# A decoder trunk whose first matmul group opens by channel tiles, with all tokens in one step

## The chip, the cores and the metric

The kernel runs on one core of a Trainium2 chip. A core has a matrix engine (TensorE, PE in the profile), a vector engine (DVE), a scalar engine (ACT), a general engine (POOL), and a queue engine (SP) that issues most transfers. Each engine works through its own instructions in the order in which they were written, and waits on semaphores for the others. The metric is the time of the program on the device in microseconds (us), lower is better.

## The reference

Two decoder layers with macaron feed-forward blocks on 512 tokens of 1024 channels, all in float32:

```
def swiglu(x, w_in, w_out):
    g, u = jnp.split(x @ w_in, 2, axis=-1)
    return (jax.nn.silu(g) * u) @ w_out

for i in range(2):
    h = h + 0.5 * swiglu(rms_norm(h, ffn1_norm[i]), ffn1_w_in[i], ffn1_w_out[i])
    hn = rms_norm(h, mix_norm[i])
    h = h + (recurrent_mixer(hn, ...) if i == 0 else spatial_gating_mixer(hn, ...))
    h = h + 0.5 * swiglu(rms_norm(h, ffn2_norm[i]), ffn2_w_in[i], ffn2_w_out[i])
return rms_norm(h, final_norm)
```

The hidden width is 2816 = 22 tiles of 128. The change concerns the first swiglu of layer 0 alone, up to the point where its hidden blocks are handed on.

## The kernel before

**Numbers in two parts.** Every float32 matmul operand is split into a rounded high part and the rest: ACT copies the high part (`hi` for activations, `whi` for weights), DVE subtracts it and keeps the rest (`lo`, `wlo`). A product is three matmuls: whi with hi, whi with lo, wlo with hi. A weight block, loaded into one of eight `raw` buffers of 128x1024, is split once by `Sub.split`; there are four buffers each for `whi` and `wlo`.

**Seven products.** Most matrix products are done on 2x2 blocks in a seven-product scheme (`seven`, lines 336 to 418): the left side has quarters A11, A12, A22, A21 (two token halves, two channel halves) and the sums S1 = A21 - A22, S2, S4, S3 formed from them on DVE. Products come in the order P1 (A11), P2 (A12), P5 (S1), P6 (S2), P3 (S4), P7 (S3), Q4 (A22), each in two steps of twelve matmuls.

**Steps.** All products of the whole kernel stand in one list, `subs`. The loop at the end (lines 1444 to 1460) goes through it; for step i it runs the work hooked to its phase "pre", splits weights some steps ahead (`ahead`, otherwise three), runs "mid" and "rest", issues loads for buffers that have come free (`load_more`), emits the step's matmuls, and then "end", the step's own follow-up and "late". This fixes the order on every engine.

**The opening.** The hidden width is dealt out as a plain pair of two tiles ("p", `pair_plain`) and chunks of four tiles (`chunk`). The pair is computed without the seven products: for each token half, A12 and A11 (or A22 and A21) times the weights. Its steps 0 to 7 are the first of the kernel: (A12, first 256 channels), (A12, second), (A11, ...), (A11, ...), then the same four weight blocks again for A22 and A21. In this opening the operands are made on the way: x is transposed on PE (`turn`, through L265), its high and low part are taken from PSUM with the gain of the norm (`parts`), and the plain value is kept for the sums (`value`). The hooks at lines 1420 to 1436 place this work, the squares for the norm (`squares`, ACT) and its reciprocal root (`rstd`: mean on DVE, root on ACT, Newton step on DVE). `first.rest(1, None)` hooks the forming and splitting of S1, S2, S4 and S3, counted from step 1. The row scale 1/rms is applied only after the matmuls, in the pair's `silu` and `post` and in the chunk's follow-ups.

Step 8 begins the chunk: P1 in steps 8 and 9, P2 in 10 and 11, P5 in 12 and 13, P6 in 14 and 15, P3 in 16 and 17, P7 in 18 and 19. When P3's second step is done, DVE makes the chunk's hidden block (two instructions `c<-C,c` and two `c<-c,rt,c`), and PE transposes it after the following step (`left_blocks`); in the profile these transposes are `e<-ident,c` of L265. Those of the pair's hidden block are `e<-ident,h`.

**Loads.** x comes by five transfers, the pair's weights by ten (the first block in halves), all from SP in the order written at lines 1355 to 1362. At most eight loads are under way, by the eight semaphores that they use in turn. P5's weights are the sum of two blocks: SP loads one, POOL adds the other by an accumulating transfer (L137).

**Before the first matmul** PE runs dummy matmuls (`warm_up`): five, and two behind each of the first two transposes.

Of the kernel before, what the change touches and what calls it, by code (L numbers as in the profile page):

```python
# [52 lines left out]
def trunk(ctx: ExitStack, tc: tile.TileContext, a: dict, out: bass.AP):  # L53
# [29 lines left out]
    def f32(t):  # L83
        return t.bitcast(F32)
# [26 lines left out]
    class Raw:  # L111


        halves = False
# [35 lines left out]
    class Sub:  # L150
# [16 lines left out]
            self.tile.used()  # L167
            self.tile = None

        def split(self, vector=False):  # L170
# [11 lines left out]
            for q in ((slice(0, 1), slice(1, 2)) if self.raw.halves else (slice(0, k),)):  # L182
                if vector:
                    nc.vector.tensor_copy(self.hi[:, q, :], src[:, q, :])
                else:
                    act(self.hi[:, q, :], src[:, q, :], AF.Copy)
                tt(self.lo[:, q, :], src[:, q, :], f32(self.hi[:, q, :]), ALU.subtract)
            if self.then is not None:
                self.raw.add(self.then)
            self.raw.used()  # L190
# [533 lines left out]
        seven(in_block(w_in, lambda n: n * DFF + f0 * P, w), [[0, 1], [2, 3]], x_left(), w,  # L724
              dict(P1=p1, P2=p2, P5=p5, P6=p6, P3=p3, P7=p7, Q4=q4), own=first, spare=aux if first else bank)

    def pair_plain(w_in, f0, group, first=False):


        w, st, ht = 2 * P, {}, {}  # L730
        raw = {}
        for k in (1, 0):
            for h in range(2):
                raw[k, h] = PairRaw(w_in, k * 512 + h * 256, f0)
                raws.append(raw[k, h])

        def bank_of(half, s):
            if (half, s) not in st:
                st[half, s] = bank("p")
            return st[half, s]  # L740

        def product(sub, half, left, h, between=None):

            sq = [(s, q) for q in range(2) for s in range(2)]
            for i, (s, q, m) in enumerate([(s, q, m) for m in range(3) for s, q in sq] if first and h else
                                          [(s, q, m) for q in range(2) for m in range(3) for s in range(2)] if first else
                                          [(s, q, m) for s, q in sorted(sq) for m in range(3)]):
                if i == 8 and between is not None:
                    between()
                z = S.z[h].hl[left][m == 1][:, q * H + s * P : q * H + (s + 1) * P]  # L750
                nc.tensor.matmul(bank_of(half, s), z, (sub.lo if m == 2 else sub.hi)[:, q, :],  # L751
                                 start=left[2] == "2" and (h, q, m) == (0, 0, 0),
                                 stop=left[2] == "1" and (h, q, m) == (1, 1, 2))

        def silu(half, s):
            t = 2 * half + s
            ht[t] = slot(name="s1")[:, :w]
            act(ht[t], st[half, s][:, :w], AF.Silu, scale=S.rt[:, t : t + 1])

        def post(half):  # L760
            for s in range(2):
                ps, t = st[half, s], 2 * half + s
                if t not in ht:
                    silu(half, s)
                o = slot(name="h")[:, :w]
                stt(o, ps[:, w:], S.rt[:, t : t + 1], ht[t], ALU.mult, ALU.mult)
                ht[t] = o
            left_blocks(group, ht, half, 7 if first else 2)

        at0 = len(subs)  # L770
        for i, (half, left) in enumerate(((0, "A12"), (0, "A11"), (1, "A22"), (1, "A21"))):
            for h in range(2):
                def mm(sub, half=half, left=left, h=h):
                    product(sub, half, left, h, opening["A11"] if first and (left, h) == ("A12", 1) else None)

                end = None
                if (left, h) == ("A11", 1):
                    end = (lambda: (hook(at0 + 7, "rest", lambda: (silu(0, 0), silu(0, 1))),
                                    hook(at0 + 8, "mid", lambda: post(0)))) if first else lambda: post(0)
                elif (left, h) == ("A21", 1):  # L780
                    end = (lambda: hook(at0 + 9, "rest", lambda: post(1))) if first else lambda: post(1)
                subs.append(Sub(raw[1 - i, h], mm, end) if i < 2 else Again(subs[at0 + 2 * (i - 2) + h], mm, end))

    class PairRaw(Raw):


        def __init__(self, w_in, r0, f0):
            super().__init__(None, [P, 2, 512])
            self.w_in, self.r0, self.f0 = w_in, r0, f0

        def fetch(self):
            for q in ((slice(0, 1), slice(1, 2)) if self.halves else (slice(0, 2),)):
                for b, base in enumerate((0, DFF)):
                    c0 = base + self.f0 * P
                    ws = self.w_in[self.r0 + q.start * P : self.r0 + q.stop * P, c0 : c0 + 256]
                    nc.sync.dma_start(out=self.v[:, q, b * 256 : (b + 1) * 256],
                                      in_=ws.rearrange("(k p) c -> p k c", p=P))

    def ffn(w_in, w_out, norm):
        f0 = 0  # L800
        for i, sizes in enumerate(FF_PARTS):
            groups, p0 = [], f0
            for n in sizes:
                if n == "p":
                    groups.append(Group(1))
                    pair_plain(w_in, f0, groups[-1], not subs)
# [556 lines left out]

    warm = cp.tile([P, T], mybir.dt.bfloat16, tag="warm", name="warm")
# [23 lines left out]
    first = BlockNorm(V_F1)  # L1388
    S.z = first.g

    def turn(i, name, where=None):
        src, _ = first.src(i, name)
        opening[i, name] = first.g[i].turn(src, where)

    def parts(i, name):
        first.g[i].direct(name, opening[i, name], first.src(i, name)[1])

    def value(i, name, vector=False):

        g, ps, gains = first.g[i], opening.pop((i, name)), first.src(i, name)[1]  # L1400
        if name == "A21" or not vector:
# [7 lines left out]
    turn(0, "A12")  # L1409
    warm_up(2, 512)  # L1410
    turn(1, "A12")
    warm_up(2, 512)
    parts(0, "A12")
    subs[0].split()
    parts(1, "A12")
    subs[1].split()
    value(0, "A12")
    value(1, "A12")
    opening["A11"] = lambda: (turn(0, "A11"), turn(1, "A11"))
    for n, phase, fn in ((0, "late", vec_rest),  # L1420
                         (2, "pre", lambda: (subs[2].split(True), parts(0, "A11"), parts(1, "A11"))),
                         (2, "pre", lambda: (subs[3].split(), value(0, "A11", True), value(1, "A11", True))),
                         (2, "end", lambda: (turn(0, "A22", bank), turn(1, "A22", bank))),
                         (3, "pre", lambda: (parts(0, "A22"), parts(1, "A22"))),
                         (3, "mid", lambda: (value(0, "A22"), value(1, "A22", True))),
                         (3, "end", lambda: (turn(0, "A21"), turn(1, "A21"))),
                         (4, "mid", lambda: (parts(0, "A21"), parts(1, "A21"))),
                         (4, "rest", lambda: (value(0, "A21"), value(1, "A21")))):
        hook(n, phase, fn)
    squares(4, "rest", "A11")  # L1430
    squares(5, "rest", "A12")
    squares(6, "rest", "A22")
    squares(6, "rest", "A21")
    rstd(6, (0, "rest"), (0, "rest"), (1, "pre"))
    first.rest(1, None)
# [51 lines left out]
```

## Time and profile before

| | us |
|---|---|
| median of 3 runs (1622.64 to 1623.0) | 1622.69 |
| the profiled execution, its time | 1622.86 |
| its span, first to last instruction | 1621.2 |
| PE busy in the span | 1608.2 |
| DVE busy | 1373.8 |
| ACT busy | 1036.8 |
| granted TensorE clock, mean | 0.999 |

How to read the rows below. The timeline gives start, length, engine, line, operation, output <- inputs and count; what stands in brackets is the engine's idle time ahead of the row and what ended it. PEld is the loading of a matmul's stationary operand. Matmuls overlap each other, so a group's length is more than its pitch times the count. The chain of waits gives start, length and what the end of the program waited for at that time; for back-to-back matmuls its pieces are the pitch. The view of stretches gives the busy time of each engine in a stretch and the number of its instructions.

### The profile page before, as it was taken

What the parts mean: (1) busy time and instruction counts of PE and PEld (TensorE: products, weight loads), DVE (VectorE), ACT (ScalarE), POOL (GpSimd) and SP (SyncE); (2) the same over time, 40 slices, a digit from 0 to 9 for tenths busy, and PEclk for the clock granted to TensorE, in tenths of its full rate; (3) what the DMA queues carried; (4) which work ended last, traced back from release to release, by engine and by line L of the source; (5) the groups of instructions that cost most, each with busy time, mean ns of one, the idle gap of its engine ahead of it and who ended that gap; (6) DMA issues with size and microseconds to landing.
All of it is one profiled execution on the core that took longest, in us unless ns stands there. A gap on an engine that the chain in (4) does not pass through costs nothing.

```text
span 1621.2 us, 20840 instructions
## 1 busy us (share of the span) xinstructions
PE 1608.2 (99%) x7451; PEld 1327.0 (82%) x7451; DVE 1373.8 (85%) x1839; ACT 1036.8 (64%) x1504; POOL 221.8 (14%) x201
## 2 busy tenths in 40 slices
PE   9999999999999999999999999999999999999998
PEld 7888888888888888888888888888888788888886
DVE  6898888888998787877887978878978988879778
ACT  7656556658776556556775565566886766565665
POOL 2111111100010111111101111111211011111110
PEclk9999999999999999999999999999999999999999
DMA  9776876943383786876838768768877557686693
GB/s 275 183 168 166 210 179 158 214 126 105 92 208 86 176 217 156 209 168 158 206 86 192 168 162 212 181 154 208 217 192 191 155 120 192 167 208 159 161 206 100
DMA packets 164695, 279.29 MB, mean 172 GB/s; under 512 B 11520, under 2 KB 38000, under 8 KB 164592
## 3 DMA queue, kind: packets, MB, share of 16 engines
q1 hardware_dynamic: 115088, 184.84, 36.2%
q0 software_dynamic: 47712, 91.30, 33.8%
q10 hardware_dynamic: 1792, 1.84, 0.4%
q8 instruction: 58, 0.95, 0.2%
q14 instruction: 45, 0.37, 0.1%
HBM read 275.84 MB, written 2.10 MB: 171 GB/s over the span
## 4 chain that ended last, share of the span: by engine, by line
PE 94%; DVE 2%; ACT 2%; issue 1%; DMA 0%; SPq 0%; DVEq 0%; ACTq 0%
PE A L365 14%; PE A L366 14%; PE A L367 14%; PE C L366 7%; PE C L367 7%; PE C L365 7%; PE p L751 5%; PE B L365 4%; PE B L367 4%; PE B L366 4%; PE e L265 3%; PE r L225 2%; PE r L223 2%; PE r L224 2%; PE Q L367 1%; PE Q L365 1%
## 5 line engine op out<-in xcount | busy, mean ns | idle before, releaser
L96 ACT ACTIVATE whi<-raw 128x1024 fp32r<-128x1024 f32 (+1 forms) x536 | 553.2, 1033 | 388.0 <-PE A L366 103.9
L87 DVE TENSOR_TENSOR wlo<-raw,whi 128x1024 fp32r<-128x1024 f32 (+1 forms) x537 | 639.7, 1194 | 181.6 <-ACT whi L96 180.3
L365 PE MATMUL A<-whi,hi 128*128 128x512 f32 x1016 | 404.1, 398 | 0.0
L367 PE MATMUL A<-wlo,hi 128*128 128x512 f32 x1016 | 396.9, 391 | 0.0
L366 PE MATMUL A<-whi,lo 128*128 128x512 f32 x1016 | 396.5, 390 | 0.0
L367 PEld LDWEIGHTS A<-wlo,hi 128*128 128x128 f32 x1016 | 190.8, 188 | 41.6 <-DVE wlo L87 0.3
L366 PEld LDWEIGHTS A<-whi,lo 128*128 128x128 f32 x1016 | 191.1, 188 | 38.6 <-DVE lo L87 0.8
L365 PEld LDWEIGHTS A<-whi,hi 128*128 128x128 f32 x1016 | 190.9, 188 | 37.5
L366 PE MATMUL C<-whi,lo 128*128 128x512 f32 x560 | 218.7, 391 | 0.9 <-DVE lo L87 0.8
L365 PE MATMUL C<-whi,hi 128*128 128x512 f32 x560 | 218.5, 390 | 0.0
L367 PE MATMUL C<-wlo,hi 128*128 128x512 f32 x560 | 218.1, 389 | 0.0
L137 POOL DMA_DIRECT2D raw<-in_ffn_w_in_dram x82 | 98.8, 1205 | 741.1 <-DVE raw L87 524.5
L137 POOL DMA_DIRECT2D raw<-in_ffn_w_out_dram x72 | 83.0, 1160 | 378.7 <-DVE wlo L87 148.7
L87 DVE TENSOR_TENSOR raw<-raw,raw 128x1024 f32<-128x1024 f32 (+1 forms) x108 | 129.7, 1201 | 1.1 <-DMA raw<-in_ffn_w_out_dram 0.6
L87 DVE TENSOR_TENSOR lo<-a,hi 128x512 fp32r<-128x512 f32 (+1 forms) x188 | 123.1, 663 | 3.7 <-ACT hi L96 3.3
L366 PEld LDWEIGHTS C<-whi,lo 128*128 128x128 f32 x560 | 105.1, 188 | 24.7 <-DVE lo L87 3.2
L96 ACT ACTIVATE hi<-a 128x512 fp32r<-128x512 f32 (+1 forms) x188 | 112.4, 601 | 17.5 <-DVE a L87 14.3
L365 PEld LDWEIGHTS C<-whi,hi 128*128 128x128 f32 x560 | 105.2, 188 | 21.8
L367 PEld LDWEIGHTS C<-wlo,hi 128*128 128x128 f32 x560 | 105.2, 188 | 21.7
L96 ACT ACTIVATE c<-A 128x512 f32<-128x512 f32 x132 | 77.4, 594 | 56.3 <-PE A L367 55.9
L365 PE MATMUL B<-whi,hi 128*128 128x512 f32 x280 | 112.1, 400 | 0.0
L367 PE MATMUL B<-wlo,hi 128*128 128x512 f32 x280 | 109.4, 391 | 0.0
(161 smaller groups left out, 2106.3 us busy)
## 6 DMA issues: line engine op xcount, KB each, us to landing
raw<-in_ffn_w_in_dram SPq DMA_DIRECT2D x162, 512.0 KB, 4.4
raw<-in_ffn_w_out_dram SPq DMA_DIRECT2D x100, 512.0 KB, 5.3
raw<-in_ffn_w_in_dram POOLq DMA_DIRECT2D x82, 512.0 KB, 7.5
raw<-in_ffn_w_out_dram POOLq DMA_DIRECT2D x60, 512.0 KB, 8.1
raw<-in_sg_w_in_dram SPq DMA_DIRECT2D x20, 512.0 KB, 6.4
raw<-in_rec_w_in_dram SPq DMA_DIRECT2D x16, 512.0 KB, 3.8
raw<-in_ffn_w_in_dram SPq DMA_DIRECT2D x30, 256.0 KB, 5.0
raw<-in_sg_w_in_dram POOLq DMA_DIRECT2D x12, 512.0 KB, 7.8
```

The costliest lines, as they stand in the source:

```text
L87: nc.vector.tensor_tensor(out=o, in0=x, in1=y, op=op)
L96: nc.scalar.activation(out=o, in_=x, func=f, **k)
L137: nc.gpsimd.dma_start(out=self.v, in_=src, accum_op=ALU.add)
L223: nc.tensor.matmul(ps, wh, xh, start=start, stop=False)
L224: nc.tensor.matmul(ps, wh, xl, start=False, stop=False)
L225: nc.tensor.matmul(ps, wl, xh, start=False, stop=stop)
L265: nc.tensor.transpose(ps[:, o : o + P], src(q, s), ident)
L365: nc.tensor.matmul(ps, zh, wh, start=fresh and i == 0, stop=False, **k)
L366: nc.tensor.matmul(ps, zl, wh, start=False, stop=False, **k)
L367: nc.tensor.matmul(ps, zh, wl, start=False, stop=end, **k)
L751: nc.tensor.matmul(bank_of(half, s), z, (sub.lo if m == 2 else sub.hi)[:, q, :], start=left[2] == "2" and (h, q, m) == (0, 0, 0), stop=lef ...
```

## The change

The opening is dealt out anew. Instead of one token half and 256 channels, a step takes one channel tile of 128 and all 512 tokens: eight steps, each with one weight block of 128x512 (gate and up half), for both token halves. The four accumulators of the pair (two per half) live through all eight steps. The channel tiles come in the order 4, 5, 6, 7, 0, 1, 2, 3, so that the two tiles of a pair of steps use the same two transposed blocks.

- Loads: x in eight transfers of 256 KB, each followed by the two transfers of 128 KB of one weight block; 24 instead of 15.
- Warm-up: five, then three and a half dummy matmuls behind the first transpose.
- `between(n)`, behind the first two matmuls of step n, makes the operands of later matmuls: the transpose of unit n+1, its parts, the split of the next weights, the value of unit n-1, and in steps 1 to 6 the squares.
- `value` is now on DVE for all quarters; the split of weights is always on ACT and DVE (one had its high part copied on DVE).
- `rstd` starts at step 7 in place of 6; `first.rest(4, None)` counts S1, S2, S4 and S3 from step 4 in place of step 1.
- The pair's Silu for all four token tiles stands in step 8 ("rest"), its product in step 9; its left blocks are handed on in four steps, 14 to 17 (A11, A12 one step earlier than before).

The cores of the diff:

```diff
-    def pair_plain(w_in, f0, group, first=False):
+    def pair_opening(w_in, f0, group):
+        ps, ht = {}, {}
+        def mm_of(n, k):
+            def mm(sub):
+                c, h, q = k // 4, k % 4 // 2, k % 2
+                for half in range(2):
+                    name = ("A11", "A12", "A21", "A22")[2 * half + c]
+                    for m in range(3):
+                        for s in range(2):
+                            if n == 0 and m == 0:
+                                ps[half, s] = bank("p")
+                            z = S.z[h].hl[name][m == 1][:, q * H + s * P : q * H + (s + 1) * P]
+                            nc.tensor.matmul(ps[half, s], z, (sub.lo if m == 2 else sub.hi)[:, 0, :],
+                                             start=(n, m) == (0, 0), stop=(n, m) == (7, 2))
+                        if (half, m) == (0, 0):
+                            opening["between"](n)
+            return mm
+        for n, k in enumerate((4, 5, 6, 7, 0, 1, 2, 3)):
+            raws.append(PairRaw(w_in, k * P, f0, 1))
+            subs.append(Sub(raws[-1], mm_of(n, k)))
+        def out(half):
+            for s in range(2):
+                pair_out(ps[half, s], 2 * half + s, ht)
+            left_blocks(group, ht, half, 5 + 2 * half)
+        hook(8, "rest", lambda: [pair_silu(ps[t // 2, t % 2], t, ht) for t in range(TT)])
+        hook(9, "pre", lambda: out(0))
+        hook(9, "mid", lambda: out(1))
```

```diff
-    raws[0].halves = True
-    load_x(0, 512, 256)
-    load_x(0, 768, 256)
-    load_more(2)
-    load_x(0, 0)
-    load_more(4)
-    load_x(2, 512)
-    load_x(2, 0)
+    UNITS = [(i, name) for c in (1, 0) for i in range(2) for name in (("A11", "A21"), ("A12", "A22"))[c]]
+    for n, (i, name) in enumerate(UNITS):
+        load_x(QUARTER[name][0], QUARTER[name][1] * 512 + i * 256, 256)
+        load_more(n + 1)
     load_more()
...
+    HOME = (aux, aux, bank, bank, aux, aux, bank, aux)
+    SQUARES = {1: [(0, 1)], 2: [(1, 1)], 3: [(2, 1)], 4: [(3, 1)], 5: [(0, 0), (1, 0)], 6: [(2, 0), (3, 0)]}
+    def between(n):
+        if n == 0:
+            turn(1)
+            parts(1, 0)
+            subs[1].split()
+            parts(1, 1)
+        elif n < 7:
+            turn(n + 1)
+            parts(n + 1, 0, 1)
+            subs[n + 1].split()
+            value(n - 1)
+            for t, c in SQUARES[n]:
+                square(t, c)
+    opening["between"] = between
+    turn(0)
+    warm_up(3, 512)
+    warm_up(1, 256)
+    parts(0, 0)
+    subs[0].split()
+    parts(0, 1)
+    hook(0, "late", vec_rest)
+    hook(7, "pre", lambda: value(6))
+    hook(7, "mid", lambda: value(7))
+    rstd(7, (0, "mid"), (0, "rest"), (1, "pre"))
+    first.rest(4, None)
-    ahead = {0: 1, 1: 1, 2: 3, 3: 3, 4: 3}
+    ahead = {0: 0, 1: 1, 2: 2, 3: 3, 4: 4, 5: 6, 6: 6, 7: 9}
```

`turn(n)` transposes unit n of `UNITS` (four transposes of 128x128) into the kind of PSUM bank that `HOME` names; `parts(n, q...)` takes the high and the low part of the 256-wide halves q, all high parts first.

More of the change, by code (lines that the diff above doesn't have):

```diff
@@ L168, in add, with split @@
             self.tile = None
-        def split(self, vector=False):
+        def split(self):
             if self.hi is not None:
@@ L181, in split @@
                 "p (k c) -> p k c", k=k)
[L182 to L187, printed above, removed]
+            act(self.hi, src, AF.Copy)
+            tt(self.lo, src, f32(self.hi), ALU.subtract)
             if self.then is not None:
@@ L733, in pair_plain @@
             for h in range(2):
-                raw[k, h] = PairRaw(w_in, k * 512 + h * 256, f0)
+                raw[k, h] = PairRaw(w_in, k * 512 + h * 256, f0, 2)
                 raws.append(raw[k, h])
[L737 to L758, printed above, removed]
+        def product(sub, half, left, h):
+            for s in range(2):
+                for q in range(2):
+                    for m in range(3):
+                        if (half, s) not in st:
+                            st[half, s] = bank("p")
+                        z = S.z[h].hl[left][m == 1][:, q * H + s * P : q * H + (s + 1) * P]
+                        nc.tensor.matmul(st[half, s], z, (sub.lo if m == 2 else sub.hi)[:, q, :],
+                                         start=left[2] == "2" and (h, q, m) == (0, 0, 0),
+                                         stop=left[2] == "1" and (h, q, m) == (1, 1, 2))
@@ L760, in post @@
         def post(half):
             for s in range(2):
[L762 to L768, printed above, removed]
+                pair_out(st[half, s], 2 * half + s, ht)
+            left_blocks(group, ht, half, 2)
         at0 = len(subs)
@@ L773, in mm @@
                 def mm(sub, half=half, left=left, h=h):
[L774 to L781, printed above, removed]
@@ L782, in pair_plain, with pair_silu @@
[L782 removed]
+                    product(sub, half, left, h)
+                end = (lambda half=half: post(half)) if (left[2], h) == ("1", 1) else None
+                subs.append(Sub(raw[1 - i, h], mm, end) if i < 2 else Again(subs[at0 + 2 * (i - 2) + h], mm, end))
+    def pair_silu(ps, t, ht):
+        ht[t] = slot(name="s1")[:, : 2 * P]
+        act(ht[t], ps[:, : 2 * P], AF.Silu, scale=S.rt[:, t : t + 1])
@@ L784, in trunk, with __init__ @@
     class PairRaw(Raw):
-        def __init__(self, w_in, r0, f0):
-            super().__init__(None, [P, 2, 512])
-            self.w_in, self.r0, self.f0 = w_in, r0, f0
+        def __init__(self, w_in, r0, f0, nk):
+            super().__init__(None, [P, nk, 512])
+            self.src = [w_in[r0 : r0 + nk * P, c0 : c0 + 256].rearrange("(k p) c -> p k c", p=P)
+                        for c0 in (f0 * P, DFF + f0 * P)]
         def fetch(self):
[L792 to L797, printed above, removed]
+            for b, src in enumerate(self.src):
+                nc.sync.dma_start(out=self.v[:, :, b * 256 : (b + 1) * 256], in_=src)
@@ L1389, in trunk, with turn, parts, value @@
     S.z = first.g
[L1391 to L1401, printed above, removed]
+    HOME = (aux, aux, bank, bank, aux, aux, bank, aux)
+    def turn(n):
+        i, name = UNITS[n]
+        opening[n] = first.g[i].turn(first.src(i, name)[0], HOME[n])
+    def parts(n, *qs):
+        i, name = UNITS[n]
+        g, ps, gains = first.g[i], opening[n], first.src(i, name)[1]
+        if 0 in qs:
+            g.hl[name] = slot(F32R, "hi"), slot(F32R, "lo")
+        hi, lo = g.hl[name]
+        for q in qs:
+            c = slice(q * H, (q + 1) * H)
+            act(hi[:, c], ps[:, c], AF.Copy, scale=gains[q])
+        for q in qs:
+            c = slice(q * H, (q + 1) * H)
+            stt(lo[:, c], ps[:, c], gains[q], f32(hi[:, c]), ALU.mult, ALU.subtract)
+    def value(n):
+        i, name = UNITS[n]
+        g, ps, gains = first.g[i], opening.pop(n), first.src(i, name)[1]
+        if name == "A21":
             g.take(name, ps, gains)
```

38 lines of the change are left out of this document (10 added, 28 removed).

## The prediction

> **What bounds the kernel now.** I read the page first, then the chain of waits and the timeline of the first 66 us, then busy time by stretch.
>
> ```profile
> span 1621.2 us, 20840 instructions
> PE 1608.2 (99%) x7451; PEld 1327.0 (82%) x7451; DVE 1373.8 (85%) x1839; ACT 1036.8 (64%) x1504; POOL 221.8 (14%) x201
> ```
>
> PE is busy throughout, so only what makes PE wait, or gives it more to do, counts. The change leaves PE's work as it is (96 matmuls of the pair, 32 transposes of x); what it can win or lose are waits. The chain of waits, from the opening and from the first chunk:
>
> ```profile
> 5.75 0.79 SPq L796
> 6.59 0.75 SPq L796
> 7.38 7.16 DMA raw<-in_ffn_w_in_dram
> 15.18 0.49 DVE lo L93
> 15.71 2.58 PE p L751 x10
> 18.30 0.87 PE e L265 x8
> 22.80 10.90 PE p L751 x48
> ...
> 53.18 0.40 PE A L367
> 64.89 0.44 PE e L265 x4
> ```
>
> Up to 15.7 us the end hangs on transfers, then on PE alone: a matmul of the pair every 0.227 us (10.90/48), a transpose every 0.109 (0.87/8). The timeline of the opening:
>
> ```profile
> 4.96 0.84 ACT L96 ACTIVATE hi<-e,vec 128x256 fp32r<-128x256 f32 x2 [2.01 <-PE e L265]
> 5.98 0.63 ACT L96 ACTIVATE whi<-raw 128x512 fp32r<-128x512 f32 x1 [0.18 <-DMA raw<-in_ffn_w_in_dram]
> 6.66 0.73 PE L751 MATMUL p<-whi,hi 128*128 128x512 f32 x2
> 10.17 1.20 PE L751 MATMUL p<-whi,hi 128*128 128x512 f32 x4 [0.47 <-ACT whi L96]
> 15.71 0.72 PE L751 MATMUL p<-whi,lo 128*128 128x512 f32 x2 [0.86 <-DVE lo L93]
> 21.76 1.04 PE L265 MATMUL e<-ident,x 128*128 128x128 f32 x8
> 22.40 1.57 ACT L96 ACTIVATE hi<-e,vec 128x256 fp32r<-128x256 f32 x4 [1.01 <-PE e L265]
> 23.27 1.66 DVE L93 SCALAR_TENSOR_TENSOR lo<-e,vec,hi 128x256 fp32r<-128x256 f32 x4 [1.18 <-ACT hi L96]
> 33.53 0.39 PE L365 MATMUL A<-whi,hi 128*128 128x512 f32 x1
> ```
>
> From the first matmul (6.66) to the chunk's first (33.53) are 26.9 us. The work in them is 96 x 0.227 = 21.8 and 24 transposes, 2.6; so PE loses 2.5 us to waits and restarts. That is all that a denser opening can win, beside an earlier start. Then busy time in the opening, and from the chunk's start to where DVE has made the chunk's first hidden half:
>
> ```profile
> 6.66:33.31 26.65, 25.24 (x120) 20.19 (x121) 19.82 (x38) 19.79 (x45) 2.48 (x2) 1.00 1.00 320
> 33.31:64.40 31.09, 31.09 (x141) 25.33 (x140) 28.78 (x42) 23.68 (x37) 5.76 (x6) 1.00 0.76 178
> ```
>
> The columns are PE, PEld, DVE, ACT, POOL, the granted clock, DMA share and GB/s. In the second stretch DVE is busy for 28.8 of 31.1 us. PE does not wait for it yet, but for the 0.40 at 53.18. So DVE work that the change moves out of the opening into this stretch has 2.3 us of room.
>
> **The change part by part: the opening.** The first weight piece was behind four loads (two of x, two of weights); now it is behind three. SP takes 0.48 us for one, so ACT's `whi` could start at 5.5 in place of 5.98; ACT is then free, as just one half of the first `hi` (0.42) stands ahead of it from 4.96. The first matmul comes 0.68 behind the start of `whi` as now: 6.2 (bounds: 6.1, when ACT is free, and 6.66, no gain). The shorter warm-up ends before that and costs nothing.
>
> Behind it lie 96 matmuls, 21.8, and 28 transposes, 3.05 (seven units of four; only the first unit comes ahead). New waits: a step takes 12 x 0.227 + 4 x 0.109 = 3.16 us. In steps 2, 4 and 6 its second half needs the unit whose transposes stand behind its own first two matmuls. By the rows, DVE's `lo` starts 1.51 us behind the first transpose (21.76 to 23.27), because it waits for both halves of `hi`, and its first piece takes 0.48: 1.99. PE has until then the four transposes (0.44), four matmuls of the first half and two with `hi` (1.36): 1.80. The wait is 0.2, and 0.1 for the restart (two matmuls in 0.72 at 15.71, where 0.39 + 0.227 = 0.62 is usual): 0.3 three times, 0.9. Per step ACT has 0.73 for `hi`, 0.53 for `whi` and 0.6 or 1.2 for squares, DVE two `lo`, one `wlo` and two values, some 2.2: both fit into 3.16, so the squares, the values and the high part that went from DVE to ACT (the 0.69 of a vector copy) cost nothing. They are hidden by PE's matmuls; without this cover, a step would be as long as ACT's 2.5.
>
> 6.2 + 21.8 + 3.05 + 0.9 = 32.0 for the chunk's first matmul, against 33.53: **1.5 us won**.
>
> **Loads.** SP issues nine more transfers, 9 x 0.48 = 4.3 us, and the chunk's loads stand behind them; all eight raw buffers are now the pair's.
>
> ```profile
> x<-in_x_dram SPq DMA_DIRECT2D x3, 512.0 KB, 7.5
> raw<-in_ffn_w_in_dram SPq DMA_DIRECT2D x6, 256.0 KB, 7.3
> x<-in_x_dram SPq DMA_DIRECT2D x2, 256.0 KB, 3.1
> raw<-in_ffn_w_in_dram SPq DMA_DIRECT2D x4, 128.0 KB, 3.6
> 24.36 1.28 POOL L137 DMA_DIRECT2D raw<-in_ffn_w_in_dram  x1 [18.18 <-DMA raw<-in_ffn_w_in_dram]
> ```
>
> These are the loads issued in the first 16 us and their medians from issue to landing. A unit is 512 KB of loads per 3.16 us, 166 GB/s, where the opening moves 320; from step 2 on loads are ahead, even at 7.5 us each. P5's first blocks wait for the buffers of steps 4 and 5 (split at about 18 and 22 us); SP's load by 7.5 and POOL's addition by another 7.5 end by 37, and the split for step 12 stands behind the Silus, at about 40. So the POOL queue, later than its 24.36, costs nothing here either; 3 us of cover.
>
> **The chunk.** Here the change puts work where there was none to spare. The rows for DVE's pitch and its idle time:
>
> ```profile
> 31.93 0.16 DVE L87 TENSOR_TENSOR ti<-ss 128x4 f32<-128x4 f32 x1 [1.15 <-ACT junk L96]
> 33.45 0.18 DVE L441 RECIPROCAL rt<-ti 128x4 f32<-128x4 f32 x1 [1.15 <-ACT ti L96]
> 34.94 1.22 DVE L87 TENSOR_TENSOR wlo<-raw,whi 128x1024 fp32r<-128x1024 f32 x1
> 36.08 0.68 DVE L87 TENSOR_TENSOR lo<-a,hi 128x512 fp32r<-128x512 f32 x1
> 36.68 0.68 DVE L87 TENSOR_TENSOR a<-a,a 128x512 f32<-128x512 f32 x1
> 69.72 1.23 DVE L87 TENSOR_TENSOR wlo<-raw,whi 128x1024 fp32r<-128x1024 f32 x1 [1.61 <-ACT whi L96]
> 34.90 1.28 ACT L96 ACT_TABLE_LOAD   x1
> 36.20 0.84 ACT L96 ACTIVATE s<-p,rt 128x256 f32<-128x256 f32 x2
> ```
>
> A `wlo` of 1024 takes 1.14 of DVE's queue, one of 512 0.60, a 256-wide piece 0.40. Five things that DVE had done before 33.31 now come behind the chunk's start: the `wlo` of P1's second block (1.14), the second S1 (0.8), the mean (0.4), `lo` of both S1 (1.2) and the first S2 (0.6). Sum 4.1; the second stretch then holds 28.8 + 4.1 = 32.9 us of DVE work.
>
> When does it begin? Unit 7's transposes stand behind two matmuls of step 6; 22 matmuls (5.0) and a wait (0.3) lie between them and the chunk, so they end at 26.7 and start at 26.3. DVE's `lo` starts at 27.8, and behind it come two `lo`, `wlo`, S1's first half, a value (3 x 0.8 + 0.6 = 3.0, to 30.8) and P1's first `wlo`, to 31.9, just in time for the third matmul at 32.4. From 31.9 DVE is behind.
>
> Its idle time has bounds 0 and 2.3, as now. I take 1.6, by ACT's queue: 0.3 for the root (the mean is ready at 31.9 + 1.14 + 0.8 + 0.4 = 34.2, and ACT stands waiting with the next two `whi` behind it), then from 34.5 on ACT has two `whi` (1.9), `hi` of S1 (0.5), a table load (1.3), four Silus (1.5) and `whi` (1.0), to 40.7, while DVE has Newton's step, two `wlo`, `lo`, two products and S2 (5.4) to 40.0: 0.7 for that and 0.6 for later `whi` of the kind that releases DVE at 69.72. So the chunk's hidden half is ready at 31.9 + 32.9 + 1.6 = 66.4; its second pair of transposes can begin at about 66.8 (the wait and PE's start), against 64.89 + 0.22 = 65.1 now. **1.7 us lost in all**, 1.5 won in the opening included: PE gives up 3.2 us between 42 and 67, in P5 (a `wlo`), P6 (both) and ahead of the chunk's transposes. Behind that DVE had 1.6 us idle at 69.72, so it catches up, and the rest runs in its old order.
>
> **The sum.** Span 1621.2 + 1.7 = 1622.9; the profiled run's own time is 1.7 above its span (1622.86), which makes 1624.6. The median of the runs is 0.17 lower: **1624.4**. With DVE's idle time between 0 and 2.3: 1622.8 to 1625.1.
>
> **Rivals.** (A) *DVE's room suffices*: another order of the same work fits, PE never waits for it, and the 1.5 us stay: 1621.2. For it: 2.3 us of idle time. Against it: 4.1 is more than 2.3, and DVE's order is fixed. (B) *Slower: loads pace the opening again.* The sixth load completes the weights of step 1; it is issued at 0.81 + 5 x 0.48 = 3.2. If it takes the 7.3 us of most loads here and not the 3.6 of the first small ones, it lands at 10.5, and step 1, which PE reaches at 6.2 + 3.16 = 9.4, begins at 11.2: 1.85 lost, 1626.25. It decides from a landing at 8.7 on. For it: the 7.3 and 7.5 of loads issued a little later. Against it: most of those had 1.5 MB or more ahead of them, this one has 0.9 MB. (C) *The clock*: PE has more short waits. In all stretches shown the granted clock is 1.00, in spite of waits of 0.47 and 0.86; one step at half of it (12 x 0.227 = 2.7 us) would take 2.7 more, which makes 1627.1. [...] (D) *It doesn't do what it says*: the warm-up of three and a half dummies ends about 0.7 before the weights; with the clock at 1.00 that changes nothing, so it has no price of its own.
>
> **How the numbers follow.** The forecast 0.60, A 0.10, B 0.25, C 0.03, others 0.02. A difference under 0.2% (3.2 us, below 1619.4 or above 1625.9) is about what a measurement of this kernel can tell from no change. Slower than that: most of B (0.20), C, and the forecast with more waits than I count (0.07): 0.30. Faster would need A and 1.8 us more: 0.03. Within: 0.67. The range reaches from A, 1621.2, to B with DVE's full idle time, 1626.25 + 0.7 and rounded up: 1627.2. The forecast's own is 1622.8 to 1625.1.
>
> **What would show it.** In the opening: the first matmul of the pair at 6.2, the chunk's first at 32.0, PE waiting for `lo` three times. In the chunk: DVE without idle time from 31 to 40 but for the root, PE held by `wlo` in P5 and P6 and by `c` ahead of `e<-ident,c`, that transpose at 66.8. If the chunk starts at 32 and PE has no such waits, A holds; if `whi` of step 1 waits for a load until past 8.7, B; granted clock under 1.00 in the first stretches, C. The prediction is wrong if PE's waits behind 70 us differ from those of before.

## The result, and the profile after

| | before | after |
|---|---|---|
| median of 21 runs each, us | 1622.81 (1622.31 to 1625.13) | 1625.05 (1624.26 to 1627.35) |
| ratio after / before | | 1.0014, 95% interval [1.0008, 1.0021] |
| span of the profiled execution, us | 1621.2 | 1623.2 |
| first matmul of the pair, us | 6.66 | 6.26 |
| first matmul of the chunk, us | 33.53 | 32.76 |
| last hidden half of the chunk begun on DVE, us | 63.69 | 65.85 |

The changed kernel is 2.24 us slower by the medians, 0.14%. It opens earlier and it loses more than it has won before 70 us. One of the eleven runs of e3, below, took 1778.08 us at a granted clock of 0.85; without it e3's median is 1622.58 in place of the 1622.73 in the table. The head of the page, and busy time by stretch (columns as before: PE, PEld, DVE, ACT, POOL, granted clock, DMA share, GB/s):

```profile
span 1623.2 us, 20863 instructions
PE 1609.8 (99%) x7451; PEld 1326.5 (82%) x7451; DVE 1375.2 (85%) x1847; ACT 1035.5 (64%) x1502; POOL 222.9 (14%) x201
...
5.86:32.00 26.14, 25.99 (x123) 20.04 (x122) 17.51 (x39) 17.04 (x41) 2.81 (x3) 1.00 0.97 292
32.00:66.50 34.50, 32.99 (x146) 25.79 (x144) 33.12 (x50) 26.06 (x41) 5.71 (x5) 1.00 0.82 195
```

The opening is dense now: PE is busy for 25.99 of 26.14 us. In the stretch behind it the two have changed places: DVE is busy for 33.12 of 34.50 us, PE for 32.99, where PE had been busy for the whole of 33.31 to 64.40 before. The view of waits says for what PE's weight loads stood still in the first 80 us; these are four of its lines (us in total, times, longest):

```profile
PEld e L258 <- DVE c L93: 1.6, 2, 1.2
PEld A L360 <- DVE wlo L87: 1.5, 2, 0.8
PEld p L781 <- DVE lo L93: 1.4, 3, 0.5
...
PEld C L360 <- DVE wlo L87: 0.3, 1, 0.3
```

One line is of the opening (three waits for `lo`), the other three are of the chunk, and all four name DVE. The longest line that does not is the wait of 0.6 us for the very first `whi`. PE in the timeline, with the transposes of x once a step, the chunk's first matmul, and its hidden block:

```profile
6.26 0.85 PE L781 MATMUL p<-whi,hi 128*128 128x512 f32 x2
13.36 0.60 PE L258 MATMUL e<-ident,x 128*128 128x128 f32 x4
16.90 0.60 PE L258 MATMUL e<-ident,x 128*128 128x128 f32 x4
20.12 0.60 PE L258 MATMUL e<-ident,x 128*128 128x128 f32 x4
32.76 0.39 PE L358 MATMUL A<-whi,hi 128*128 128x512 f32 x1
50.37 0.50 PE L360 MATMUL A<-wlo,hi 128*128 128x512 f32 x1 [0.42 <-DVE wlo L87]
53.91 0.50 PE L360 MATMUL A<-wlo,hi 128*128 128x512 f32 x1 [0.25 <-DVE wlo L87]
66.66 0.55 PE L258 MATMUL e<-ident,c 128*128 128x128 f32 x3 [1.00 <-DVE c L93]
```

A step with a wait takes 16.90 - 13.36 = 3.54 us, one without 20.12 - 16.90 = 3.22. DVE's timeline, from the last unit's `lo` on:

```profile
28.46 0.88 DVE L93 SCALAR_TENSOR_TENSOR lo<-e,vec,hi 128x256 fp32r<-128x256 f32 x2 [1.64 <-ACT hi L96]
29.25 0.68 DVE L87 TENSOR_TENSOR wlo<-raw,whi 128x512 fp32r<-128x512 f32 x1
...
31.42 2.36 DVE L87 TENSOR_TENSOR wlo<-raw,whi 128x1024 fp32r<-128x1024 f32 x2
33.69 0.87 DVE L93 SCALAR_TENSOR_TENSOR s<-e,vec,a 128x256 f32<-128x256 f32 x2
34.48 0.16 DVE L87 TENSOR_TENSOR ti<-ss 128x4 f32<-128x4 f32 x1
...
35.11 0.18 DVE L434 RECIPROCAL rt<-ti 128x4 f32<-128x4 f32 x1 [0.27 <-ACT ti L96]
...
39.32 0.88 DVE L93 SCALAR_TENSOR_TENSOR h<-p,rt,s 128x256 f32<-128x256 f32 x2 [0.30 <-ACT s L96]
41.36 1.23 DVE L87 TENSOR_TENSOR wlo<-raw,whi 128x1024 fp32r<-128x1024 f32 x1 [0.57 <-ACT whi L96]
...
65.85 0.75 DVE L93 SCALAR_TENSOR_TENSOR c<-c,rt,c 128x512 f32<-128x512 f32 x1
...
71.59 1.23 DVE L87 TENSOR_TENSOR wlo<-raw,whi 128x1024 fp32r<-128x1024 f32 x1 [1.31 <-ACT whi L96]
```

Between 31.42 and 71.59 only three rows have idle time ahead of them: 0.27, 0.30 and 0.57, together 1.14 us, all for ACT. ACT shows why:

```profile
32.08 1.28 ACT L96 ACT_TABLE_LOAD   x1
34.87 0.20 ACT L96 ACTIVATE ti<-ti 128x4 f32<-128x4 f32 x1 [1.51 <-DVE ti L90]
34.98 1.99 ACT L96 ACTIVATE whi<-raw 128x1024 fp32r<-128x1024 f32 x2
...
37.52 1.28 ACT L96 ACT_TABLE_LOAD   x1
38.81 1.57 ACT L96 ACTIVATE s<-p,rt 128x256 f32<-128x256 f32 x4
40.25 1.08 ACT L96 ACTIVATE whi<-raw 128x1024 fp32r<-128x1024 f32 x1
```

ACT stands for 1.51 us, because the mean (`ti<-ss`, 0.16 us of work) is queued on DVE behind two `wlo` and a value; the root, two `whi`, the table load and four Silus then come that much later, and DVE waits for them in turn. The chain of waits from 49 us on:

```profile
49.18 1.14 DVE wlo L87
...
53.91 0.50 PE A L360
...
65.21 0.61 DVE c L87
65.85 0.76 DVE c L93
66.66 0.55 PE e L258 x3
```

In this place the chain of before held nothing but PE. The next transposes of `e<-ident,c` began at 67.95 before; now they begin at 69.82, a shift of 1.87 of the 2.0 by which the spans differ.

### The profile page after: what moved, and what is told of

Read it like the earlier page. It is cut to its first block, busy times and chain, and to the rows that moved or that the text cites. A ratio compares the mean times of both kernels' runs of the same rounds, so it can differ in the third digit from the quotient of the medians.

```text
span 1623.2 us, 20863 instructions
## 1 busy us (share of the span) xinstructions
PE 1609.8 (99%) x7451; PEld 1326.5 (82%) x7451; DVE 1375.2 (85%) x1847; ACT 1035.5 (64%) x1502; POOL 222.9 (14%) x201
## 4 chain that ended last, share of the span: by engine, by line
PE 92%; DVE 4%; ACT 3%; issue 1%; DMA 1%; DVEq 0%; ACTq 0%
PE A L358 13%; PE A L360 13%; PE A L359 13%; PE C L359 7%; PE C L360 7%; PE C L358 7%; PE p L737 4%; PE B L358 4%; PE B L360 4%; PE B L359 4%; PE e L258 3%; PE r L218 2%; PE r L217 2%; PE r L216 2%; PE Q L358 1%; PE Q L360 1%
```

## The experiments

The theory, **DVE-late**: from the last unit's `lo` to the chunk's last `c` DVE works through a fixed queue, and the length of that queue, counted from that `lo`, sets when PE goes on. Its refinement, **ACT-chain**: the 1.14 us of idle time in that queue come from the late mean. Rivals: the amount of DVE's work counts, wherever it stands; DVE is full from the opening on; PE's own work.

All runs in one table. The experiments ran in three groups, each with its own runs of the kernel before (medians 1623.01 beside e1 to e4, 1622.88 beside e5 to e8, 1623.01 beside e9 to e12); "against after" is the kernel's distance to these, less 2.24. The last column is DVE's queue in the profile, from the start of the last unit's `lo` to the start of the chunk's last `c`, less the 65.85 - 28.46 = 37.39 us of the changed kernel.

| kernel | median, us | span, us | ratio to before [95%] | against after, us | queue against after, us |
|---|---|---|---|---|---|
| e1 transposes and splits ahead of the matmuls | 1624.39 | 1622.5 | 1.0010 [1.0001, 1.0018] | -0.86 | 0.00 |
| e2 mean first | 1623.82 | 1621.3 | 1.0004 [0.9995, 1.0012] | -1.43 | -1.44 |
| e3 both | 1622.73 | 1620.3 | 0.9998 [0.9989, 1.0008] | -2.52 | -1.41 |
| e4 after, 1.8 us of DVE added in step 9 | 1627.23 | 1625.6 | 1.0026 [1.0016, 1.0036] | +1.98 | +1.82 |
| e5 before, the same in step 9 | 1624.50 | 1622.8 | 1.0010 [1.0001, 1.0019] | | |
| e6 before, the same in step 6 | 1622.59 | 1620.5 | 0.9999 [0.9990, 1.0008] | | |
| e7 after, the same in steps 2, 4, 5 | 1625.08 | 1623.6 | 1.0014 [1.0005, 1.0023] | -0.04 | +0.06 |
| e8 after without the pair's products | 1624.39 | 1624.1 | 1.0010 [1.0000, 1.0019] | -0.73 | -0.77 |
| e9 splits one step earlier | 1623.40 | 1621.6 | 1.0001 [0.9992, 1.0010] | -1.85 | -1.75 |
| e10 all three edits | 1621.24 | 1619.4 | 0.9989 [0.9980, 0.9998] | -4.01 | -2.91 |
| e11 as e10, one split moved alone | 1621.73 | 1619.8 | 0.9992 [0.9983, 1.0001] | -3.52 | -3.03 |
| e12 two Silus a step later | 1624.48 | 1623.0 | 1.0008 [1.0000, 1.0017] | -0.77 | -0.65 |

The intervals are wide beside these steps (0.0009 is 1.5 us). What makes the table readable is that two columns of different origin, a median over eleven runs (eight in e4) and one length in one profile, agree within 0.2 us wherever PE's order in the opening was left as it is (e2, e4, e7, e8, e9, e12). Besides, no run of the changed kernel lies under 1624.26, and none of e2, e9, e10 or e11 lies above 1624.11. The steps of e1, e8 and e12, 0.73 to 0.86, are smaller than the scatter of single runs; for e8 and e12 the queue bears them out. Spans are of one execution each and carry what it lost or won at its start (the last section), 1.6 us in e8.

**e1: transposes and splits ahead of the step's matmuls.**

```diff
+                if n:
+                    opening["between"](n)
                 for half in range(2):
...
-                        if (half, m) == (0, 0):
+                        if (half, m, n) == (0, 0, 0):
                             opening["between"](n)
```

> The changed kernel, but from step 1 on the next unit's transposes, its splits, its values and its squares are issued ahead of the step's first two matmuls, not behind them. Theory DVE-late (the chunk's start is fed by a DVE queue that itself follows PE's transposes in the opening; the time is lost where PE waits for that queue): PE's three waits for lo (0.33 each) go, the chunk's first matmul moves from 32.76 to about 31.8, DVE's queue comes forward with it, and the span falls by about 1.0 us, 1623.2 to 1622.2. Rival DVE-full (DVE has no free moment in the opening either, so it reaches the chunk no earlier): the chunk's first matmul moves by 1.0 all the same, PE waits 1.0 longer for wlo and c between 41 and 67, and the span stays at 1623.2.

PE's three waits for `lo` are gone, and the steps take 3.21 us throughout. The median falls by 0.86. The chunk's first matmul stands at 32.48 and not at 31.8, and the profiled time is 0.7 lower and not 1.0, because this execution lost 0.7 us at the very start (last section): from the pair's first matmul to the chunk's it takes 32.48 - 6.37 = 26.11 us, and e3, whose PE has the same order, 31.41 - 6.00 = 25.41. DVE's queue has the same 37.39 us to the hundredth; it begins 0.41 earlier and ends 0.41 earlier. So DVE is not full in the opening: it follows PE's transposes there, and what PE gains is kept. DVE-full falls.

**e2: the mean first; e3: both edits.**

```diff
-    rstd(7, (0, "mid"), (0, "rest"), (1, "pre"))
+    rstd(7, (0, "pre"), (0, "rest"), (1, "pre"))
```

> The changed kernel with one DVE operation moved: the mean of the squares (0.16 us) stands at the head of step 7's work, ahead of the two wlo and the last unit's value, so that ACT gets it some 2.5 us earlier for the root. Theory ACT-chain (from 32 to 41 us the limit is not DVE's amount of work, but ACT, which stands 1.51 us waiting for that mean and then has its root, two whi, a table load and four Silus ahead of DVE's products): DVE's idle 0.30 and 0.57 at 39.32 and 41.36 goes, the last c of the first half starts 0.9 to 1.2 earlier than 65.85, and the span falls by 0.9 to 1.2, to about 1622.1. Rival DVE-amount (4.1 us of moved DVE work against 2.3 of room, an order doesn't matter): at most the 0.27 at the root goes, the span stays within 0.3 of 1623.2.

> Both edits together: next unit's transposes and splits ahead of the step's first matmuls, and the mean at the head of step 7's DVE work. If both limits exist and lie one behind the other (DVE-late with ACT-chain), the gains add: span 1623.2 - 1.0 - 1.1 = about 1621.1, no slower than the kernel before (1621.2). If only one of them is real, the span is that of the better single edit, 1622.2. If neither is, 1623.2.

In e2 one instruction of 0.16 us (and the constant added behind it) stands 3.2 us earlier. DVE's and ACT's timelines of e2:

```profile
31.31 0.15 DVE L87 TENSOR_TENSOR ti<-ss 128x4 f32<-128x4 f32 x1
...
34.64 0.17 DVE L434 RECIPROCAL rt<-ti 128x4 f32<-128x4 f32 x1
...
38.44 0.87 DVE L93 SCALAR_TENSOR_TENSOR h<-p,rt,s 128x256 f32<-128x256 f32 x2
...
39.82 1.22 DVE L87 TENSOR_TENSOR wlo<-raw,whi 128x1024 fp32r<-128x1024 f32 x1
...
64.30 0.75 DVE L93 SCALAR_TENSOR_TENSOR c<-c,rt,c 128x512 f32<-128x512 f32 x1
```

```profile
33.27 0.21 ACT L96 ACTIVATE ti<-ti 128x4 f32<-128x4 f32 x1
```

No bracket is left on these rows: reciprocal, product and `wlo` start without a wait, and the last `c` comes 1.55 earlier. The instructions of DVE are the same. So 1.4 of the 2.2 us lost were the order of one small instruction; DVE-amount, which allowed 0.3, falls. Of the 1.44 by which the queue is shorter, 1.14 are the three waits; the other 0.30 are busy time (36.01 us in the changed kernel's queue, 35.71 in that of e2), for which no row shown gives the cause. e3 adds both gains (0.86 + 1.43 = 2.29 against 2.52 measured, 2.67 without its long run): with them the changed opening is level with the kernel before.

**e4, e5, e6, e7: the same dose of DVE work in four places.** Three additions of 512 wide, their result unused:

```diff
+    def dose(k):
+        for _ in range(k):
+            j = slot(name="dose")
+            tt(j, X[:, 0, :512], X[:, 0, :512], ALU.add)
+    hook(9, "rest", lambda: dose(3))
```

(e4 and e5; in e6 `hook(6, "rest", ...)`, in e7 one `dose(1)` each in `between(2)`, `between(4)` and `between(5)`; e6 and e7 have a tile filled on POOL as source.)

> The changed kernel with three more DVE additions of 512 wide (0.60 us of the queue each, 1.8 in all, their result unused) in step 9, behind the first of the moved work. Theory DVE-late: from 41 us on DVE has no idle time, so all of it is passed on: the last c of the first half starts 1.8 later (67.65), PE waits 1.8 longer ahead of the chunk's transposes, span 1625.0. Rival (PE's time is lost to something else, and DVE has room): span 1623.2, within 0.3.

> The kernel before with the same three additions (1.8 us of DVE's queue, result unused) in step 9 as in the last run. Theory DVE-late: the 2.3 us of idle time that DVE has there between 33.31 and 64.40 are waits for ACT and for the root at its beginning, ahead of the dose, and no room behind it; so the dose is passed on as in the changed kernel, less what DVE is ahead of PE at 64.89 (some 0.2): span 1621.2 + 1.6 to 1.8 = about 1622.9. Rival room (2.3 us of idle time absorb 1.8 of work wherever it stands): span 1621.2, within 0.3.

> The kernel before with the same three additions in step 6 instead, still in the opening, where DVE has idle time (19.82 busy of 26.65) and ahead of its waits for the mean and the root. Theory DVE-late: most of it is absorbed there, span 1621.2 to 1621.8. Rival amount (what counts is DVE's work up to the chunk's transposes, wherever it stands): 1.6 to 1.8 more, as in the run before, 1622.9.

> The changed kernel with the same three additions, one each behind steps 2, 4 and 5 of the opening. Theory DVE-late: DVE has idle time in the opening (17.5 busy of 26.1) between PE's transposes, so 1.8 us there cost little, span 1623.2 to 1623.7. Rival DVE-full (DVE is behind from the opening on): all is passed on, 1625.0.

In step 9 the dose costs 1.98 us in the changed kernel and 1.62 in the kernel before (1624.50 - 1622.88); in the steps of the opening it costs nothing (-0.29 in e6, -0.04 in e7). The kernel before had the 2.3 us of idle time in the same stretch, and yet had no room in step 9. PE in e5 says where it stopped:

```profile
48.28 0.50 PE L367 MATMUL C<-wlo,hi 128*128 128x512 f32 x1 [0.74 <-DVE wlo L87]
51.76 0.50 PE L367 MATMUL A<-wlo,hi 128*128 128x512 f32 x1 [0.46 <-DVE wlo L87]
```

Of DVE's waits in the kernel before, 0.66 lies ahead of the dose (38.02) and 0.68 and 0.51 behind it (55.56, 58.43); the last two are still there in e5, 1.6 later, for they too wait for ACT. My expectation had all of the idle time ahead of the dose; that was wrong in the place, and the price came out as expected because PE already waits at 48 and 52, ahead of the later idle time. DVE's timeline of e6 shows where the room was:

```profile
31.49 1.89 DVE L87 TENSOR_TENSOR dose<-dz 128x512 f32<-128x512 f32 x3
33.29 0.17 DVE L441 RECIPROCAL rt<-ti 128x4 f32<-128x4 f32 x1
...
37.30 1.22 DVE L87 TENSOR_TENSOR wlo<-raw,whi 128x1024 fp32r<-128x1024 f32 x1
```

Though hooked to step 6, the dose runs at the end of the opening and across the chunk's start (32.81 in e6). It stands between the mean and the root, where the kernel before waited 1.15 for ACT, and ahead of the wait of 0.66 for `whi`; both brackets are gone. So e6 does not show that the opening as such has room (e7 does, for the changed kernel), but that the dose is free when it stands ahead of these waits, and e5 that a step behind them it is not. Idle time of an engine is room only for work that may stand where the idle time is.

**e8: without the pair's products.**

```diff
         def out(half):
-            for s in range(2):
-                pair_out(ps[half, s], 2 * half + s, ht)
             left_blocks(group, ht, half, 5 + 2 * half)
```

> The changed kernel without the four products of the pair's result (Silu's half times the other half), 1.6 us of DVE at 39 to 42 us; it leaves out this part of the computation, the left blocks take Silu's output. Theory DVE-late with ACT-chain: behind 41 us DVE's queue sets the end, but its waits for ACT's chain ahead of the products stay, and grow by part of what is left out, so half of it comes back: span 1622.0 to 1622.6. Rival DVE-amount: all of 1.6 comes back, 1621.6. Rival PE-own (the lost time isn't DVE's): 1623.2.

Four products, 0.79 us for each two, 1.58 in all, are left out, and 0.73 comes back. DVE in e8 has one row that pays for the rest:

```profile
43.26 1.22 DVE L87 TENSOR_TENSOR wlo<-raw,whi 128x1024 fp32r<-128x1024 f32 x1 [1.74 <-ACT whi L96]
```

Its wait for `whi` has grown from 0.57 to 1.74, while the 0.30 for Silu is gone: 1.58 - (1.74 - 0.57 - 0.30) = 0.71. At 39 to 43 us ACT sets the pace, as ACT-chain has it; behind that DVE does.

**e9: splits earlier; e12: two Silus later.**

```diff
-    ahead = {0: 0, 1: 1, 2: 2, 3: 3, 4: 4, 5: 6, 6: 6, 7: 9}
+    ahead = {0: 0, 1: 1, 2: 2, 3: 3, 4: 5, 5: 7, 6: 8, 7: 9}
```

```diff
-        hook(8, "rest", lambda: [pair_silu(ps[t // 2, t % 2], t, ht) for t in range(TT)])
+        hook(8, "rest", lambda: [pair_silu(ps[0, t], t, ht) for t in range(2)])
+        hook(9, "rest", lambda: [pair_silu(ps[1, t], 2 + t, ht) for t in range(2)])
...
-            left_blocks(group, ht, half, 5 + 2 * half)
+            left_blocks(group, ht, half, 5 + half)
...
-        hook(9, "mid", lambda: out(1))
+        hook(10, "mid", lambda: out(1))
```

> The changed kernel with weight splits put earlier in the opening: the pair's sixth and eighth block one step earlier, P1's first block in step 6 in place of step 7. Of DVE's work this takes one wlo of 1024 (1.14 us) from behind the chunk's start into DVE's idle time of the opening, and the mean, which stood behind it, comes 1.14 earlier too. Theory DVE-late: 1.1 us of the 2.2 lost come back, the last c of the first half starts at 64.7 in place of 65.85 and the median goes from 1625.05 to about 1623.9. Rival opening-full (ACT and DVE have no room in the opening, the added whi and wlo delay hi and lo of the last unit): the chunk's first matmul comes up to 0.9 later than 32.76 and nothing is won, 1625.0.

> The changed kernel with two of the four Silus, and the second half's product and left blocks, one step later (steps 9 and 10 in place of 8 and 9). Theory ACT-chain: at 39 to 41 us DVE waits for ACT (0.30 and 0.57); with two Silus of 0.37 behind the next whi, that whi comes 0.7 earlier and some 0.6 of DVE's wait goes: 1624.3 to 1624.5. Rival DVE-amount: the amount of work is the same, 1625.0.

e9 wins 1.85 where I expected 1.1. I had counted P1's first `wlo` (1.14) and overlooked that the eighth block's `wlo` (0.60, the row at 29.25) stood behind the last `lo` too; 1.74 together, and the queue is 1.75 shorter. It does this in spite of the same idle 0.27, 0.30 and 0.57, so e9 takes work out of the queue, and e2 idle time. e12 wins 0.77: of the three waits the 0.57 ahead of the `wlo` is gone, 0.27 and 0.29 stay, which is what ACT-chain gave for it.

**e10, e11: three edits.** e3 with the `ahead` of e9; in e11 with `5: 6, 6: 8, 7: 9`.

> All three edits: next unit's transposes and splits ahead of the step's first matmuls, the mean at the head of step 7's DVE work, and the weight splits earlier as in the run before. Theory DVE-late with ACT-chain: the gains still add, since DVE stays behind from the chunk's start to its transposes: from 1622.73 (the first two) some 1.1 to 1.6 more, 1621.1 to 1621.6, faster than the kernel before (1622.9) by 1.3 to 1.8. Rival (with two edits DVE has caught up, the rest is PE's own work): 1622.7.

> As the run before, but of the splits only P1's first block is put earlier (step 6), so that DVE's and ACT's work for the last unit stands behind it. Theory DVE-late: one wlo of 1.14 out of the chunk, less a wait of PE for the last unit's lo in step 7 (up to 0.5): 1621.5 to 1622.1. Rival as before: 1622.7.

e10 runs in 1621.24 us, 1.77 below the kernel before, ratio 0.9989 [0.9980, 0.9998], and 1.49 below e3 (1.34 without the long run of e3). That is less than the 1.85 of e9; DVE's queue is 1.50 shorter than that of e3, and its chain of waits shows that DVE no longer sets the pace:

```profile
26.79 5.49 PE p L783 x24
62.35 0.23 PE A L360
63.27 0.44 PE e L258 x4
```

From the opening to the hidden block the chain holds PE alone again, as in the kernel before. DVE's queue is short enough, and the gain of the opening is kept. e11 is between e3 and e10 (its one wait for `lo` in the opening is 0.5).

## Why the prediction was right, point by point

**The opening: the step was right, its size was not.** The term "3.16 us a step, 0.3 three times, first matmul at 6.2" gave 32.0; measured are 6.26 and 32.76, so 0.77 was won where 1.5 was forecast. From 6.26 to 32.76 are 26.50 us against 25.8. Of the difference, 0.3 lies in the matmul's pitch (twelve in 2.76 to 2.77 in the chain of after, 0.230 each and not 0.227: 96 x 0.003), 0.1 in the three waits (3.54 - 3.22 = 0.32 each, forecast 0.3), and 0.3 in the first two matmuls, which took 0.77 in the chain where two take 0.46 (last section). The waits came in steps 2, 4 and 6 as said.

**DVE's ledger: right in sum, by two terms that were off against each other.** P1's first `wlo` was to end at 31.9; it ends at 31.42 + 1.14 = 32.56, which is the opening's error handed on. Idle time was taken as 1.6 and is 1.14. The work of 32.9 us is what stands between: 66.6 (the last `c`, 65.85 + 0.75) - 32.56 - 1.14 = 32.9. Forecast for that `c` were 66.4. On PE, from the chunk's first matmul to the next transposes of `e<-ident,c`, it took 69.82 - 32.76 = 37.06 us against 67.95 - 33.53 = 34.42: 2.64 lost where 3.2 was forecast, and 0.77 won where it was 1.5. The total hangs on when DVE ends, not on when PE opens, and DVE ended 0.2 late: 0.66 handed on by the opening, less 0.46 of idle time that was assumed and did not come. That these two nearly cancel is luck.

**The mechanism** is shown by e4, e5, e6 and e7: 1.8 us of DVE work cost 1.98 and 1.62 in step 9 of the two kernels, and nothing in the opening (e7) or ahead of DVE's waits at its end (e6). That the five moved pieces (4.1 us) are the cause follows from the ledger (DVE is busy for 32.66 us from 32.56 to 66.60, against 28.78 in the stretch of before); e9 moved two others, P1's first `wlo` and the eighth block's, and got them back in full (1.75). Of the five, only the mean was moved back, in e2, and there its place counted and not its 0.4. P1's second `wlo`, the second S1, the `lo` of both S1 and the first S2 were not, so their share is worked out and not measured.

**What the ledger did not see** is that a part of its idle time was not a property of the work but of one place: "0.3 for the root" and "0.7 for Silu" were put down to ACT's queue, and ACT's queue was late because the mean was queued behind two `wlo` and a value. So the sign "DVE without idle time from 31 to 40 but for the root" did not come: DVE waits 0.30 for Silu at 39.32. I had the row of that wait in the sum ("ACT stands waiting") and priced it at 0.3; e2 shows 1.4.

**Rival A** (DVE's room suffices) falls with e5: the room was not where the work is. **Rival B** (loads) falls with the trace: ACT takes step 1's weights at 7.96, ahead of the 8.7 from which loads would have decided, and does not wait:

```profile
7.96 0.62 ACT L96 ACTIVATE whi<-raw 128x512 fp32r<-128x512 f32 x1
```

The loads are not far ahead, though: in e2 the same row stands at 8.12, behind a wait of 0.16 for its transfer.

**Rival C** (the clock fails between short waits) falls by the pitch of the matmuls behind such waits: 0.23 to 0.24 each in the chain of after behind the wait of 1.00 ahead of 66.66, and the same in that of e5 behind 0.46. No run shows its term of 2.7 us, the clock fallen to half behind a short wait: in the changed kernel the record of the granted clock has full speed from 6.54 to 1617.63 us, through all of PE's waits there, and half pace is seen ahead of that, from the first dummy on (last section). **Rival D** was given no price, and that was wrong: see the last section. PE's shift at the next transposes is 1.87, and of the 2.0 between the spans little came later, as forecast: from 70 to 150 us PE is busy for 79.66 us in both kernels.

## What to carry to other kernels

Denser work in one stage can move its side work into the next (here DVE's 28.78 us behind the opening became 32.66): before counting the gain, follow the queue of the helper engine from the last thing that must be done to the first thing that is waited for, in order, and sum it. Idle time of that engine is room only ahead of the instruction that waits (here 1.8 us of work cost nothing there, in e6, and 1.62 behind it, in e5). Look in such a queue for a small instruction on which a long chain of another engine hangs (here a mean of 0.16 us, worth 1.4), and put it first.

## What the runs showed of the hardware that was not expected

**PE begins at half pace, and when that ends differs from run to run.** The first five dummy matmuls start 0.42 us apart ((2.94 - 1.26)/4 in the kernels before and after), where the pair's matmuls, as wide, follow each other by 0.23 later on. The fifth starts at 2.94 in the ten profiles of before, after and e1 to e8, yet the first two matmuls of the pair take 0.72 in some of them and 1.22 in others. Half pace lasted longest in e8; in e3 it was one of the shortest. PE in the timeline of each, e8 first:

```profile
6.60 1.22 PE L781 MATMUL p<-whi,hi 128*128 128x512 f32 x2 [0.27 <-ACT whi L96]
7.62 1.05 PE L258 MATMUL e<-ident,x 128*128 128x128 f32 x4
8.33 1.20 PE L781 MATMUL p<-whi,lo 128*128 128x512 f32 x2
...
10.18 0.64 PE L781 MATMUL p<-whi,hi 128*128 128x512 f32 x2
```

```profile
4.62 0.93 PE L1382 MATMUL warm<-warm 128*128 128x512 bf16 x4
6.00 0.72 PE L783 MATMUL p<-whi,hi 128*128 128x512 f32 x2 [0.45 <-ACT whi L96]
```

In e8 the half pace lasts to 10.2 us (0.43 a matmul from 9.33 to 10.18, 0.24 behind it), and from the first matmul of the pair to the chunk's it takes 34.70 - 6.60 = 28.10 us, 1.6 more than in the changed kernel, whose opening is otherwise the same; this execution took 1626.06 where the median of its kernel is 1624.39. In e3 the dummies behind the first transposes run at full pace from 4.62 on, four in 0.93 us. Five of the eleven profiles of the new opening (e1, e7, e8, e9, e12) have two or more of the pair's matmuls at half pace. In the kernel before the first matmul comes at 6.66, and in e5 and e6, which open like it, the half pace ended at about 6.4; in these three profiles it fell on dummies and transposes. So an earlier start can pay for this from the 0.77 it wins. That the kernel before is spared is not shown by three profiles: in e1, e7, e9 and e12 the pair's first two matmuls went at half pace up to 7.39, 7.29, 7.07 and 7.49, and that would have met its first matmuls too.

The column of the granted clock does not show it. It reads 1.00 in e8 for the very microsecond in which matmuls run at half pace (columns here: PE's busy time, granted clock, DMA share, GB/s):

```profile
8.00:9.00 1.00, 1.00 (x6) 1.00 1.08 370
```

The trace behind the column does, in the kernels before and after. Its record of the granted clock has no entry ahead of the change to full speed, and the column takes a time without an entry as 1.00. The first entry stands at 5.57 us in the kernel before and 6.54 in the changed one, just where the pitch of the matmuls changes. From there on the record has full speed without a break for 1611.09 us in both, until 1616.66 and 1617.63, and 0.50 behind that. My prediction took the clock to be 1.00 before the weights came and so left the dummies out of the account; in the changed kernel the half pace reached into the first two matmuls, which is the 0.3 of them above. By the pitch, the change comes between 4.6 us (e3) and 10.2 (e8). What sets its moment, and why e8's came so late, is not shown.

**The first load varies too.** In e10 PE waits 1.23 us for the first `whi`, which waits for its transfer and starts at 6.01, and in e3, where it starts at 5.32, 0.45: the first matmul of the same opening stands at 6.69 and at 6.00. Profiles of single executions differ by that much at the start, which is why the table counts DVE's queue from an event inside.
